# A hand-written order for the first stretch of a mixer kernel: loads, layer norms and the first projection on three engines

## The chip, the cores and the metric

The kernel runs on one core of one Trainium2 chip. The metric is the device time of one launch in microseconds (us), the median of several runs; smaller is better.

## The reference, cut to what matters

One layer: a token mixer (HGRN2 and GLA scans over 512 latent and 256 context tokens of width 1024), then a PEER expert layer. The change touches only the way to the first scan:

```python
m_l = jax.nn.silu(c) @ w_ada[i] + b_ada[i]
m_c = jax.nn.silu(c_ctx) @ w_ada[i] + b_ada[i]
...
u_l = modulate(x, sh1_l, sc1_l) @ w_in[i]     # modulate: layer_norm(x) * (1 + scale) + shift
u_c = modulate(xc, sh1_c, sc1_c) @ w_in[i]
```

The latent tokens x and the context tokens xc are normalized, scaled and shifted by the modulation columns, and projected by w_in.

## The kernel before, in words

`Net.mixer` opens with a stretch that ends when the first head unit's projections are begun; the body (project, scan) follows. Six token blocks of 128 rows (4 of x, numbers 2 to 5, and 2 of ctx, numbers 0 and 1) go through `first_norm`: a load into one of 4 buffers `xin` (L280), statistics on VectorE (L119, L125), the inverse deviation `rsa` by two ScalarE activations (L127, L128), the normalization on VectorE (L283), 8 TensorE transposes into two PSUM tiles `pT` (L288), two ScalarE copies to `xt` (L289). `mods_first` computes the modulation columns `m1` in 4 groups of 256 columns of shift and scale: 4 weight loads of 512 KB per group (`wada1`, 8 buffers, L173), 8 matmuls into `pmr` (L178), a VectorE copy `mrow` (L180), 4 tiny matmuls `pm` (L183), the sum with the bias column `b1` (L185). The bias is a load of 8 KB (L167), to whose scale half VectorE adds 1 (L168). `modulate_first` makes the input's high and low halves `hTh` (ScalarE, L296) and `hTl` (VectorE, L298, L299) for two of 8 slices k per group, latent and context apart. `w_slab` splits a weight slab `wraw` in the same way into `wh` (ScalarE, L308) and `wl` (VectorE, L309). `begin` multiplies, for each k, the latent tokens (2 matmuls of 512 columns into `pr`, 12 of 256 into `pt`) and the context tokens (5 of 256) with the first token slabs; after it the Z transposes (L364) and the first slab projection `pc` run. `scan_consts` makes masks and lower bounds for the scans.

Order: all engines work off their own queue in order. In this stretch of the kernel before, a list scheduler chose the order on each engine from the dependences. Loads are issued by SP, all on one queue, and each load waits for a semaphore of one of 8 lanes: it is issued only when the load eight before it has landed.

Of the kernel before, what the change touches and what calls it, by code (L numbers as in the profile page):

```python
# [21 lines left out]
TC = 256  # L22
# [9 lines left out]
class Net:  # L32
    def __init__(self, tc, a):
        self.tc, self.nc, self.a = tc, tc.nc, a

# [17 lines left out]
    def scan_consts(self, c, tmp):  # L53
        nc, a = self.nc, self.a

        si = tmp.tile([128, 64], I32, name="si")
# [19 lines left out]

        z = c.tile([128, 2, 4], F32, name="lbz")
        nc.sync.dma_start(z, a["hg_lb"])
# [17 lines left out]

        self.w2 = c.tile([64, 2, 256], F32, name="w2")
        nc.vector.memset(self.w2, 0.0)
        for i in (0, 32):
            nc.sync.dma_start(self.w2[i:i + 16, 0, :], a["w_gk2"][0])  # L100
            nc.sync.dma_start(self.w2[i + 16:i + 32, 1, :], a["w_gk2"][1])
        self.bgk = c.tile([128, 2, 2], F32, name="bgk")
        nc.sync.dma_start(self.bgk, a["b_gk"])
# [41 lines left out]
    def mods_first(self, pers, pool, ps):  # L145

        nc, a = self.nc, self.a
        t1 = pool.tile([128, 8, 2], F32, name="cct1")  # L150
        t2 = pool.tile([128, 8, 2], F32, name="cct2")
        sil = pool.tile([128, 8, 32], F32, name="sil")
        sc = sil[:, :, 0:2]
        nc.vector.memset(sil, 0.0)
        self.log_sigmoid(sc, self.cc, t1, t2)
        nc.scalar.activation(sc, sc, AF.Exp)
        nc.vector.tensor_tensor(sc, sc, self.cc, op=OP.mult)

        si = pool.tile([128, 2], I32, name="seli")
        nc.gpsimd.iota(si, pattern=[[-1, 2]], base=0, channel_multiplier=1)  # L160
        nc.vector.tensor_scalar(si, si, 31, None, op0=OP.bitwise_and)
        sel = pool.tile([128, 2], F32, name="sel")
        nc.vector.tensor_copy(sel, si)
        nc.vector.tensor_scalar(sel, sel, 0.0, None, op0=OP.is_equal)
        self.m1 = pers.tile([128, 16, 2], F32, name="m1")
        bias = pool.tile([128, 4, 2, 2], F32, name="b1")
        nc.sync.dma_start(bias, a["b1col"])  # L167
        nc.vector.tensor_scalar(bias[:, :, 1], bias[:, :, 1], 1.0, None, op0=OP.add)  # L168
        for g in range(4):
            yield  # L170
            ws = [pool.tile([128, 2, 512], F32, name="wada1", bufs=8) for _ in range(4)]
            for i, w in enumerate(ws):
                nc.sync.dma_start(w, a["w_ada1"][g][:, i * 2:i * 2 + 2])  # L173
            yield
            p = ps.tile([128, 512], F32, name="pmr", bufs=1)
            for k in range(8):
                j = k % 4 * 32
                nc.tensor.matmul(p[j:j + 32, :], sil[:, k, :], ws[k // 2][:, k % 2, :], start=k < 4, stop=k > 3)  # L178
            mrow = pool.tile([128, 512], F32, name="mrow", bufs=2)
            nc.vector.tensor_copy(mrow, p)  # L180
            pm = ps.tile([128, 4, 2], F32, name="pm", bufs=1)
            for m in range(4):
                nc.tensor.matmul(pm[:, m, :], mrow[:, m * 128:(m + 1) * 128], sel, start=m == 0, stop=m == 3)  # L183
            for i in range(2):
                nc.vector.tensor_tensor(self.m1[:, 8 * i + 2 * g:8 * i + 2 * g + 2], pm[:, 2 * i:2 * i + 2],  # L185
                                        bias[:, g, i, :, None].to_broadcast([128, 2, 2]), op=OP.add)

# [88 lines left out]
    def first_norm(self, pool, ps, xt, b):  # L276
# [6 lines left out]
        nc.vector.tensor_scalar(x, x, mu, rs, op0=OP.subtract, op1=OP.mult)  # L283
        for g in range(2):
# [6 lines left out]
    def modulate_first(self, pool, xt, ks, *parts):  # L291
        nc = self.nc
        for k in ks:
            for i, j, s in parts:
                sc, sh = self.m1[:, 8 + k, s:s + 1], self.m1[:, k, s:s + 1]
                nc.scalar.activation(self.hTh[:, k, i:j], xt[:, k, i:j], AF.Identity, bias=sh, scale=sc)  # L296
                h = pool.tile([128, T], F32, name="hT", bufs=3)[:, :j - i]
                nc.vector.tensor_scalar(h, xt[:, k, i:j], sc, sh, op0=OP.mult, op1=OP.add)  # L298
                nc.vector.tensor_tensor(self.hTl[:, k, i:j], h, self.hTh[:, k, i:j], op=OP.subtract)  # L299


    def w_slab(self, src):
        shape = [128] + list(src.shape[1:])
        raw = self.wp.tile(shape, F32, name="wraw", bufs=2)
        self.nc.sync.dma_start(raw, src)
# [4 lines left out]
        return hi, lo  # L310

    def token_slabs(self, u):
        return [self.w_slab(self.a["w_tf"][u, :, i * 4:(i + 1) * 4, :]) for i in range(2)]
# [280 lines left out]
    def begin(self, u, ps, slabs, wr):  # L594
# [7 lines left out]
        for k in range(8):  # L602
            wh, wl = (t[:, k % 4, :] for t in slabs[k // 4])
            ctx = lambda: self.mm3(both[:, 0, :], wh[:, 0:128], wl[:, 0:128], self.hTh[:, k, 0:TC], self.hTl[:, k, 0:TC],
                                   k == 0, k == 7)
            if k < 7:
                ctx()
            for p, sl in ((pc, slice(0, TC)), (pl, slice(TC, TA))):
                for i, h in enumerate((self.hTh, self.hTl)):
                    nc.tensor.matmul(p, wr[:, k, :], h[:, k, sl], start=p is pl and k + i == 0,  # L610
                                     stop=p is pl and k + i == 8)
            if k == 7:
                ctx()
# [4 lines left out]
            if k % 2:  # L618
                yield
# [149 lines left out]
    def mixer(self, es):  # L769
# [13 lines left out]
        with tc.tile_pool(name="first", bufs=1) as fp, tc.tile_pool(name="fps", bufs=2, space=PSUM) as fps:  # L783
# [6 lines left out]
            mods = self.mods_first(self.c, fp, fps)  # L790
            norm = [self.first_norm(fp, fps, xt, b) for b in (2, 3, 4, 5, 0, 1)]
            step = lambda *gens: [next(g, None) for g in gens]
            lat, ctx = (TC, TA, 0), (0, TC, 1)
            step(*norm[:4], mods, mods)
            self.scan_consts(self.mp, fp)
            step(norm[0], norm[1], norm[4], norm[5])
            raw = fp.tile([128, 8, 32], F32, name="wr")
            nc.sync.dma_start(raw, self.a["w_r"])
            slabs = self.token_slabs(seq[0])
            wr = fp.tile([128, 8, 64], F32R, name="wrs")  # L800
            nc.scalar.activation(wr[:, :, 0:32], raw, AF.Copy)
            nc.vector.tensor_tensor(wr[:, :, 32:64], raw, wr[:, :, 0:32], op=OP.subtract)
            self.ahead = {}
            begin = self.begin(seq[0], fps, slabs, wr)
            step(norm[2], norm[3], mods, mods)
            self.modulate_first(fp, xt, range(0, 2), lat)
            step(norm[4], norm[5])
            self.modulate_first(fp, xt, range(0, 2), ctx)
            for g in (1, 2, 3):
                step(mods, begin, mods)  # L810
                self.modulate_first(fp, xt, range(2 * g, 2 * g + 2), lat, ctx)
            step(begin, begin)
# [5 lines left out]
        LEAD = 1.145  # L818
        while proj:
            if pp < ps + LEAD:  # L820
                pp = advance(proj, pp)
            elif m2 and pm < ps:
                m2 = m2 if next(m2, None) else None
# [557 lines left out]
```

## Time and profile before

| what | value |
|---|---|
| median of 3 runs (lowest, highest) | 1765.1 us (1762.88, 1768.2) |
| the profiled execution's own time | 1758.76 us |
| its span, first to last instruction | 1756.6 us |
| mean granted TensorE clock, share of full | 0.987 |
| TensorE matmul busy in the span | 97% |
| VectorE, ScalarE busy in the span | 82%, 47% |

The timelines below give for each instruction (or merged run of equal ones) its start from the span's beginning, its duration, engine, line, operation, output and inputs; in square brackets stands the engine's idle time before it and what ended it. Matmuls are pipelined: the next one starts before the shown end of the last, so the distance of two starts is the price of one.

### The profile page before, as it was taken

The numbers are of one execution on the slowest core, as the hardware profiler recorded it, in microseconds if no ns is written. First come the engines' busy times: TensorE is split into PE (matmuls) and PEld (weight loads), VectorE is DVE, ScalarE is ACT, GpSimd is POOL, SyncE is SP. The second block draws the span as 40 slices with busy tenths as digits, with TensorE's granted clock in tenths as the row PEclk, the third lists the DMA queues.
The fourth block names the chain that finished last, engine by engine and source line by source line (L and its number), as shares of the span: only waits on it lengthen the run. The fifth ranks groups of instructions, "written<-read, shape, count | busy, mean of one in ns | idle before, by whom it ended". The sixth has DMA issues, their size and how long they took to land. (4 is left out here: it accounts for less than half of the span.)

```text
span 1756.6 us, 28197 instructions
## 1 busy us (share of the span) xinstructions
PE 1699.8 (97%) x10501; PEld 1486.9 (85%) x10501; DVE 1447.2 (82%) x2917; ACT 833.2 (47%) x1417; POOL 406.7 (23%) x286
## 2 busy tenths in 40 slices
PE   6999999989999999999999999999999999999997
PEld 3888877877778999999998999999999998888886
DVE  6688988877779999999996878777777786776768
ACT  4677677655133355676674333333333333333332
POOL 0000000000023102238422544443444342111000
PEclk8999999999989999999999999999999999999999
DMA  8444435242322257989999999989999989999862
GB/s 321 122 127 162 139 96 182 95 179 101 108 73 85 73 152 290 332 298 322 332 333 355 368 341 351 323 304 334 325 309 338 321 299 309 351 332 305 270 217 96
DMA packets 174811, 428.99 MB, mean 244 GB/s; under 512 B 14993, under 2 KB 78801, under 8 KB 170578
## 3 DMA queue, kind: packets, MB, share of 16 engines
q1 hardware_dynamic: 137234, 290.87, 48.5%
q0 software_dynamic: 36864, 134.23, 21.8%
q8 instruction: 82, 1.34, 0.3%
q10 hardware_dynamic: 576, 2.10, 0.3%
q14 instruction: 55, 0.45, 0.1%
HBM read 378.38 MB, written 48.76 MB: 243 GB/s over the span
## 5 line engine op out<-in xcount | busy, mean ns | idle before, releaser
L139 PE MATMUL pH<-hh,uh 128*128 128x384 f32 x1024 | 350.3, 342 | 1.1 <-ACT gels L1111 1.1
L141 PE MATMUL pH<-hh,ul 128*128 128x384 f32 x1024 | 347.7, 340 | 1.5 <-DVE ul L1098 1.5
L140 PE MATMUL pH<-hl,uh 128*128 128x384 f32 x1024 | 347.0, 339 | 0.0
L139 PE MATMUL y<-vh,ah 128*128 128x512 f32 x768 | 302.8, 395 | 2.9 <-ACT ah L1137 2.9
L140 PE MATMUL y<-vl,ah 128*128 128x512 f32 x768 | 301.5, 393 | 0.1
L141 PE MATMUL y<-vh,al 128*128 128x512 f32 x768 | 301.5, 394 | 0.0
L1098 DVE TENSOR_TENSOR vl<-vr,vh 128x1024 fp32r<-128x1024 f32 x128 | 156.7, 1224 | 151.7 <-ACT vh L1096 150.7
L1167 POOL DMA_INDIRECT erow<-in_u_dram,ix x128 | 187.8, 1467 | 370.4 <-DVE scr L1176 219.1
L1167 POOL DMA_INDIRECT erow<-in_v_dram,ix x128 | 185.4, 1448 | 327.3 <-DVE yg L1184 179.8
L1096 ACT ACTIVATE vh<-vr 128x1024 fp32r<-128x1024 f32 x128 | 135.1, 1057 | 195.2 <-issue 125.9
L1137 ACT ACTIVATE ah<-gel 128x384 fp32r<-128x384 f32 x128 | 66.8, 524 | 276.6 <-DVE gel L1134 273.6
L139 PEld LDWEIGHTS pH<-hh,uh 128*128 128x128 f32 x1024 | 192.4, 188 | 3.8 <-ACT gels L1111 1.4
L140 PEld LDWEIGHTS pH<-hl,uh 128*128 128x128 f32 x1024 | 192.8, 188 | 2.7
L141 PEld LDWEIGHTS pH<-hh,ul 128*128 128x128 f32 x1024 | 192.4, 188 | 2.6 <-DVE ul L1098 2.4
L1096 ACT ACTIVATE uh<-ur 128x1024 fp32r<-128x1024 f32 x128 | 135.0, 1056 | 121.2 <-PE pH L140 75.3
L141 PEld LDWEIGHTS y<-vh,al 128*128 128x128 f32 x768 | 144.9, 189 | 33.6
L139 PEld LDWEIGHTS y<-vh,ah 128*128 128x128 f32 x768 | 144.7, 188 | 33.0 <-ACT ah L1137 3.4
L140 PEld LDWEIGHTS y<-vl,ah 128*128 128x128 f32 x768 | 144.9, 189 | 30.6 <-DVE vl L1098 0.5
L1098 DVE TENSOR_TENSOR ul<-ur,uh 128x1024 fp32r<-128x1024 f32 x128 | 155.6, 1216 | 16.0 <-PE pH L141 13.9
L1184 DVE SCALAR_TENSOR_TENSOR yg<-erow,act,yg 128x1024 f32<-128x1024 f32 x127 | 162.2, 1277 | 0.1
L1176 DVE SCALAR_TENSOR_TENSOR scr<-erow,h 128x1024 bf16<-128x1024 f32 x128 | 155.8, 1218 | 0.0
L139 PE MATMUL pc<-hTh,wh 128*128 128x512 f32 (+1 forms) x304 | 109.5, 360 | 0.9 <-ACT V L407 0.7
(367 smaller groups left out, 3047.0 us busy)
## 6 DMA issues: line engine op xcount, KB each, us to landing
ur<-in_uT_dram SPq DMA_DIRECT2D x128, 512.0 KB
vr<-in_v_dram SPq DMA_DIRECT2D x128, 512.0 KB
Gd<-stage SPq DMA_DIRECT2D x24, 1024.0 KB
Gn<-Gd SPq DMA_DIRECT2D x16, 1536.0 KB
wraw<-in_w_cf_dram SPq DMA_DIRECT2D x24, 512.0 KB
wada<-in_w_ada_dram SPq DMA_DIRECT2D x48, 256.0 KB
Hd<-gels SPq DMA_DIRECT2D x56, 192.0 KB
gel<-Hd SPq DMA_DIRECT2D x56, 192.0 KB
```

The lines of the kernel that those rows point to most:

```text
L139: mm(out, lh, rh, start=start, stop=False)
L140: mm(out, lh, rl, start=False, stop=False)
L141: mm(out, ll, rh, start=False, stop=stop)
L1096: nc.scalar.activation(hi, raw, AF.Copy)
L1098: sub = eng.tensor_tensor(lo, raw, hi, op=OP.subtract)
L1137: nc.scalar.activation(ah, g, AF.Copy)
L1167: nc.gpsimd.indirect_dma_start(out=e, out_offset=None, in_=a[src], in_offset=bass.IndirectOffsetOnAxis(ap=self.ix[:, j:j + 1], axis=0))
L1176: nc.vector.scalar_tensor_tensor(scr, e, 1.0, h2, op0=OP.mult, op1=OP.mult, accum_out=dots[:, j:j + 1])
L1184: nc.vector.scalar_tensor_tensor(y, e, act[:, j:j + 1], y, op0=OP.mult, op1=OP.add)
```

## The change

TensorE, VectorE and ScalarE follow the program's own order in the stretch (`manual_schedule`), and the program is rewritten step by step. Loads: the raw vector `wr` and the two first token slabs are issued straight behind the four x blocks, and the bias and the modulation weights behind them; the second ctx block and parts of `scan_consts` move among the weights. `begin` hands out two functions, `latent(k)` and `context(k)`, which the program calls as the columns become ready. Both slabs are split before the first modulation group is copied. The masks and bounds of `scan_consts` come after the modulation of latent slices 2 and 3. `modulate_first` makes all high halves and products first and the low halves after them. The first 8 body steps are held behind the last of these instructions and loads. The rest of the kernel is the same.

```diff
@@ mods_first
-        for g in range(4):
-            yield
+        def load(g):
             ws = [pool.tile([128, 2, 512], F32, name="wada1", bufs=8) for _ in range(4)]
...
+        loaded = [load(0)]
+        yield
+        loaded.append(load(1))
+        yield
+        for g in range(4):
+            ws = loaded[g]
...
@@ modulate_first
-                nc.vector.tensor_tensor(self.hTl[:, k, i:j], h, self.hTh[:, k, i:j], op=OP.subtract)
+                todo.append((self.hTl[:, k, i:j], h, self.hTh[:, k, i:j]))
+        for out, h, high in todo:
+            lo = nc.vector.tensor_tensor(out, h, high, op=OP.subtract)
@@ mixer
-            step(*norm[:4], mods, mods)
-            self.scan_consts(self.mp, fp)
...
+            with tc.manual_schedule(engines={*engines}):
+                step(*(norm[b] for b in (2, 3, 4, 5)))
+                raw = fp.tile([128, 8, 32], F32, name="wr")
+                nc.sync.dma_start(raw, self.a["w_r"])
+                raws = self.token_raws(seq[0])
+                mods = self.mods_first(self.c, fp, fps)
+                consts = self.scan_consts(self.mp, fp)
+                wr = fp.tile([128, 8, 64], F32R, name="wrs")
+                step(mods, norm[2], norm[2], norm[3], norm[3], consts)
+                step(norm[4], norm[0], norm[1], mods)
...
+                step(norm[4], norm[5])
+                slabs = [self.split(raws[0])]
+                step(mods, norm[5])
...
+                slabs.append(self.split(raws[1]))
+                begin = self.begin(seq[0], fps, slabs, wr)
+                latent, context = next(begin)
+                step(mods, mods)
+                mod((0, 1), lat)
+                step(norm[0], norm[1])
+                latent(0)
+                latent(1)
+                step(norm[0], norm[1])
+                mod((0, 1), ctx)
+                step(mods, mods)
+                context(0)
+                context(1)
+                step(mods)
+                mod((2, 3), lat)
+                step(consts)
+                mod((2, 3), ctx)
+                latent(2)
+                step(mods)
+                latent(3)
...
+                for k in (6, 7):
+                    latent(k)
+                    context(k)
```

Three places of the built program, first the queue of loads on SP, from its start. Before:

```order
L785 DMA cc<-in_ccol_dram 128x16
L280 DMA xin<-in_x_dram 128x1024 x4
L167 DMA b_130<-in_b1col_dram 128x16
L173 DMA wada_133<-in_w_ada_dram 128x1024
L173 DMA wada_134<-in_w_ada_dram 128x1024
```

Now:

```order
L822 DMA cc<-in_ccol_dram 128x16
L294 DMA xin<-in_x_dram 128x1024 x4
L835 DMA wr<-in_w_r_dram 128x256
L329 DMA wraw<-in_w_tf_dram 128x1024 x2
L169 DMA b_139<-in_b1col_dram 128x16
L174 DMA wada_142<-in_w_ada_dram 128x1024
```

The bias `b` stood right behind the x blocks and now stands behind `wr` (128 KB) and two slabs of 512 KB.

VectorE up to the second normalization (`sel` is a small constant, `sta` and `mva` the statistics). Before, the bias (L168) stood behind the second normalization:

```order
L119 BN_STATS sta<-xin 128x6
L64 CAST xf<-xo 128x64
L283 TENSOR_SCALAR xin<-xin,mva,rsa 128x1024
L168 TENSOR_SCALAR b_130<-b_130 128x4x2
L69 TENSOR_SCALAR mlo<-xf 128x64
```

Now:

```order
L166 TENSOR_SCALAR sel<-sel 128x2
L170 TENSOR_SCALAR b_139<-b_139 128x4x2
L121 BN_STATS sta<-xin 128x6 x2
L127 BN_AGGR mva<-sta 128x2
L297 TENSOR_SCALAR xin<-xin,mva,rsa 128x1024
L121 BN_STATS sta<-xin 128x6 x2
L127 BN_AGGR mva<-sta 128x2
L297 TENSOR_SCALAR xin<-xin,mva,rsa 128x1024
```

The instruction on the bias now heads the statistics of all blocks.

ScalarE over the x blocks. Before, the deviation of the second block (L127, L128) stood ahead of the first block's copies (L289):

```order
L127 ACTIVATE rsa<-mva,eps 128x1
L128 ACTIVATE rsa<-rsa 128x1
L127 ACTIVATE rsa<-mva,eps 128x1
L128 ACTIVATE rsa<-rsa 128x1
L289 ACTIVATE xt<-pT 128x4x128 x2
```

Now:

```order
L129 ACTIVATE rsa<-mva,eps 128x1
L130 ACTIVATE rsa<-rsa 128x1
L304 ACTIVATE xt<-pT 128x4x128 x2
L129 ACTIVATE rsa<-mva,eps 128x1
L130 ACTIVATE rsa<-rsa 128x1
L304 ACTIVATE xt<-pT 128x4x128 x2
```

Each block's deviation now stands behind the copies of the block before it.

## Rows read from the trace of the kernel before

**Rows 1.** Windows: start:end, length, busy (count) of PE, PEld, DVE, ACT, POOL; PEclk, DMA.

```profile
26.50:31.40 4.90, 4.90 (x20) 2.64 (x20) 3.50 (x6) 2.83 (x6) 0.00 (x0) 0.50 1.02 400
...
64.70:90.10 25.40, 25.40 (x146) 22.38 (x146) 19.32 (x37) 20.36 (x31) 0.00 (x0) 1.00 0.63 185
90.10:93.00 2.90, 0.47 (x3) 0.19 (x2) 2.90 (x7) 2.90 (x7) 0.00 (x0) 0.98 0.18 30
93.00:96.40 3.40, 3.40 (x17) 3.40 (x18) 3.40 (x6) 1.14 (x4) 0.00 (x0) 0.52 0.74 232
```

**Rows 2.** Timeline of TensorE in the stretch and at its end.

```profile
8.68 4.02 PE L288 MATMUL pT<-ident,xin 128*128 128x128 f32 x16 [8.68 <-DVE ident L47]
...
14.46 1.09 PE L288 MATMUL pT<-ident,xin 128*128 128x128 f32 x8
...
26.49 1.97 PE L288 MATMUL pT<-ident,xin 128*128 128x128 f32 x8 [6.06 <-DVE xin L283]
...
40.77 1.06 PE L178 MATMUL pmr<-wada,sil 128*32 128x512 f32 x8
...
46.30 0.95 PE L183 MATMUL pm<-sel,mrow 128*128 128x2 f32 x8
...
48.14 0.39 PE L610 MATMUL pr<-hTh,wrs 128*64 128x512 f32 x1
...
48.60 0.28 PE L139 MATMUL pt<-wh,hTh 128*128 128x256 f32 x1
48.72 0.29 PE L140 MATMUL pt<-wl,hTh 128*128 128x256 f32 x1
...
64.68 0.50 PE L139 MATMUL pc<-hTh,wh 128*128 128x512 f32 x1 [0.25 <-ACT G L376]
```

**Rows 3.** Timeline of SP: the issues of the 13th, 15th and 16th load.

```profile
8.83 0.32 SPq L101 DMA_DIRECT2D w<-in_w_gk_dram  x1
...
10.75 0.31 SPq L101 DMA_DIRECT2D w<-in_w_gk_dram  x1
12.04 0.35 SPq L103 DMA_DIRECT2D bgk<-in_b_gk_dram  x1
```

**Rows 4.** DMA packets of two stretches: first 3.1 to 7.8 us, then 7.8 to 9.2.

```profile
DMA packets 512, 1.90 MB, mean 404 GB/s; under 512 B 48, under 2 KB 48, under 8 KB 512
...
DMA packets 271, 0.46 MB, mean 331 GB/s; under 512 B 160, under 2 KB 160, under 8 KB 271
```

**Rows 5.** Timeline of VectorE in the stretch.

```profile
4.87 1.29 DVE L119 BATCH_NORM_STATS2 sta<-xin 128x6 f32<-128x512 f32 x2 [0.97 <-DMA xin<-in_x_dram]
...
7.04 0.80 DVE L283 TENSOR_SCALAR xin<-xin,mva,rsa 128x1024 f32<-128x1024 f32 x1
...
11.31 0.20 DVE L70 SCALAR_TENSOR_TENSOR mask<-xf,mlo 128x64 uint8<-128x64 f32 x1
...
14.82 0.81 DVE L283 TENSOR_SCALAR xin<-xin,mva,rsa 128x1024 f32<-128x1024 f32 x1
...
18.63 0.69 DVE L180 COPY mrow<-pmr 128x512 f32<-128x512 f32 x1 [2.38 <-PE pmr L178]
...
20.65 0.11 DVE L185 TENSOR_TENSOR m<-pm,b 128x4 f32<-128x4 f32 x1
...
21.92 0.68 DVE L299 TENSOR_TENSOR hTl<-hT,hTh 128x512 fp32r<-128x512 f32 x1
...
30.07 1.23 DVE L309 TENSOR_TENSOR wl<-wraw,wh 128x1024 fp32r<-128x1024 f32 x1 [1.36 <-ACT wh L308]
...
34.38 0.91 DVE L299 TENSOR_TENSOR hTl<-hT,hTh 128x256 fp32r<-128x256 f32 x2 [0.24 <-ACT hTh L296]
```

**Rows 6.** Timeline of ScalarE in the stretch.

```profile
6.43 0.29 ACT L127 ACTIVATE rsa<-mva,eps 128x1 f32<-128x1 f32 x1 [2.74 <-DVE mva L125]
...
10.69 0.60 ACT L289 ACTIVATE xt<-pT 128x512 f32<-128x512 f32 x1 [0.25 <-PE pT L288]
...
28.99 1.05 ACT L308 ACTIVATE wh<-wraw 128x1024 fp32r<-128x1024 f32 x1
```

More of the change, by code (lines that the diff above doesn't have):

```diff
@@ L310, in w_slab, with token_raws @@
         return hi, lo
+    def token_raws(self, u):
+        return [self.raw_slab(self.a["w_tf"][u, :, i * 4:(i + 1) * 4, :]) for i in range(2)]
     def token_slabs(self, u):
-        return [self.w_slab(self.a["w_tf"][u, :, i * 4:(i + 1) * 4, :]) for i in range(2)]
+        return [self.split(raw) for raw in self.token_raws(u)]
     def proj_c(self, slab, out_l, out_c, colmajor=False, scale=1.0):
@@ L601, in begin, with latent @@
         self.ahead[u] = [both[:, 0, :], *vg]
-        for k in range(8):
+        def latent(k):
             wh, wl = (t[:, k % 4, :] for t in slabs[k // 4])
[L604 to L613, printed above, removed]
+            for i, h in enumerate((self.hTh, self.hTl)):
+                nc.tensor.matmul(pl, wr[:, k, :], h[:, k, TC:], start=k + i == 0, stop=k + i == 8)
             for b in range(2, 6):
@@ L617, in begin, with context, value @@
                          k == 0 and b % 2 == 0, k == 7 and b % 2 == 1)
-            if k % 2:
-                yield
+        def context(k):
+            wh, wl = (t[:, k % 4, 0:128] for t in slabs[k // 4])
+            def value():
+                self.mm3(both[:, 0, :], wh, wl, self.hTh[:, k, 0:TC], self.hTl[:, k, 0:TC], k == 0, k == 7)
+            if k < 7:
+                value()
+            for h in (self.hTh, self.hTl):
+                nc.tensor.matmul(pc, wr[:, k, :], h[:, k, 0:TC], start=False, stop=False)
+            if k == 7:
+                value()
+        yield latent, context
         nc.scalar.activation(self.rT[:, TC:].rearrange("p (c r) -> p c r", r=8),
@@ L789, in mixer @@
             seq = (0, 1, 4, 2, 5, 3)
-            mods = self.mods_first(self.c, fp, fps)
-            norm = [self.first_norm(fp, fps, xt, b) for b in (2, 3, 4, 5, 0, 1)]
+            lat, ctx = (TC, TA, 0), (0, TC, 1)
+            mod = lambda ks, part: self.modulate_first(fp, xt, ks, part)
             step = lambda *gens: [next(g, None) for g in gens]
-            lat, ctx = (TC, TA, 0), (0, TC, 1)
-            step(*norm[:4], mods, mods)
-            self.scan_consts(self.mp, fp)
-            step(norm[0], norm[1], norm[4], norm[5])
@@ L797, in mixer @@
[L797 to L812, printed above, removed]
+            norm = {b: self.first_norm(fp, fps, xt, b) for b in range(6)}
+            engines = (mybir.EngineType.PE, mybir.EngineType.DVE, mybir.EngineType.Activation)
@@ new lines, in mixer @@
+            with tc.manual_schedule(engines={*engines}):
[8 more added lines that the diff above has]
+                step(norm[4], norm[0], norm[1], mods)
+                nc.scalar.activation(wr[:, :, 0:32], raw, AF.Copy)
+                step(norm[4], norm[5])
+                slabs = [self.split(raws[0])]
+                step(mods, norm[5])
+                nc.vector.tensor_tensor(wr[:, :, 32:64], raw, wr[:, :, 0:32], op=OP.subtract)
+                slabs.append(self.split(raws[1]))
+                self.ahead = {}
+                begin = self.begin(seq[0], fps, slabs, wr)
[17 more added lines that the diff above has]
+                latent(3)
+                step(mods)
+                context(2)
+                context(3)
+                step(mods)
+                mod((4, 5), lat)
+                mod((4, 5), ctx)
+                step(mods)
+                latent(4)
+                step(mods)
+                latent(5)
+                step(mods)
+                context(4)
+                context(5)
+                mod((6, 7), lat)
+                mod((6, 7), ctx)
+                for k in (6, 7):
+                    latent(k)
+                    context(k)
@@ L813, in mixer @@
+            step(begin)
         self.up = pool(el, "unit")
@@ L818, in mixer @@
         LEAD = 1.145
+        behind = 8
         while proj:
-            if pp < ps + LEAD:
+            if behind:
+                behind -= 1
+                with self.behind():
+                    pp = advance(proj, pp)
+            elif pp < ps + LEAD:
                 pp = advance(proj, pp)
             elif m2 and pm < ps:
-                m2 = m2 if next(m2, None) else None
+                with self.behind():
+                    m2 = m2 if next(m2, None) else None
                 pm += 0.165
```

51 lines of the change are left out of this document (36 added, 15 removed).

## The prediction

> **What bounds the kernel now.** I read the busy times by stretch first: from 64.7 to 90.1 us, the start of the body, TensorE is busy 25.40 of 25.40 us at full clock [rows 1]. So whatever moves the first slab projection `pc`, which starts at 64.68 [rows 2], moves the body behind it, and the question is when `pc` starts after the change. Then I read the timelines of the four queues ahead of it. TensorE: 16 transposes as soon as the first blocks are normalized (8.68), an idle gap of 6.06 us before the ctx transposes at 26.49, and after that hardly a gap up to 64.68 [rows 2]. That gap is what an order by hand could win, with the half clock behind it: from 26.5 to 31.4 the granted clock was 0.50 (1.2 GHz) [rows 1]; 8 transposes took 1.97 us there and 1.09 at 2.4 GHz [rows 2]. VectorE: statistics of the first block at 4.87, as soon as it has landed, normalizations at 7.04 and, the fourth, 14.82; first modulation columns done at 20.76 (20.65 + 0.11) [rows 5]. SP: a load is issued when the load eight before it has landed, so these issues date landings: the 13th at 8.83 is the landing of the fourth x block, the 15th and 16th at 10.75 and 12.04 are landings of two weight loads of 512 KB, 1.29 us apart [rows 3].
>
> **The change, step by step.** I follow the chain of what waits for what on the new order, with durations from rows.
>
> *1. The bias load.* It now stands behind `wr` and two slabs, and the VectorE instruction that adds 1 to it heads the statistics of every block. One queue serves its loads in order: before, the bias was issued at 3.08 behind the x blocks. In 3.1 to 7.8 us only 48 packets under 512 B moved, in the much shorter 7.8 to 9.2 us 160 [rows 4]. The bias is 128 small packets, so they moved with the end of the last x block. Now it lands at 8.83 plus a quarter of 1.3 for `wr`, two times 1.3 for the slabs and 0.2 for itself: 12.0. VectorE, which took its first statistics at 4.87, starts them at 12.0. All x blocks have been there since 8.83.
>
> By the Trainium skill's page "DMA: Bandwidth & Descriptors", section "Queues, rings and completion order", completion is not first-in first-out per issuing engine, so a small load could finish ahead of large ones; rows 4 speak against it here. By that rule step 1 would cost nothing (the first rival).
>
> *2. Four normalizations in series.* The first follows the statistics as before: 12.0 + (7.04 - 4.87) = 14.2 [rows 5]. For the others ScalarE's order decides: the deviation of a block now stands behind the copies of the block before it, and those wait for the transposes, which wait for the normalization. A period is: normalization 0.80 [rows 5], 8 transposes, second copy 0.60, two activations 0.29 + 0.20 [rows 6], four handovers of about 0.1. With transposes at half clock (4.02 / 2 = 2.0 [rows 2]) that is 4.2 to 4.3 us, at full clock (1.09) 3.3. I take 4.2, because TensorE comes from idle and has 2 us of work in each period; 3.3 is kept as the low end. The fourth normalization starts at 14.2 + 3 x 4.2 = 26.8 and ends at 27.6, where it started at 14.82 before.
>
> *3. To the first modulation columns.* Now both slabs are split ahead of `mrow`. Behind the fourth normalization: 8 transposes and second copy 1.9 (29.5; at half clock 0.9 more), `wh` of the second slab on ScalarE 1.05 [rows 6], `wl` 1.23, `mrow` 0.69 [rows 5], `pm` 0.95 [rows 2], sums 0.2 and handovers: columns at 33.8, 13.0 us later than the 20.76 of before. The weights land by about 17.2 (12.0 + 4 x 1.3), so they no longer set anything.
>
> *4. From the columns to* `pc`. Prices: latent(k) two starts of 0.23 (48.14 to 48.60) and 12 of 0.12 = 1.9; context(k) 5 x 0.12 = 0.6; four `pmr` matmuls 1.06 [rows 2]; columns to first low half 1.8 (20.76 to 22.60) [rows 5].
> - low half of slice 0 at 35.5. latent(0), latent(1): 3.8, plus 1.5 for a part at half clock, since TensorE was idle from about 29.7 (between 0 and the 2.4 that 4.9 us at half clock cost from 26.5 [rows 1]): 40.8.
> - The ctx norms start when VectorE is through the low halves (36.1) and take 3.0 each in series: 42.0. Second ctx transposes to 43.1, eight `pmr` to 45.2, context(0), (1) to 46.4, `pm` behind `mrow` to 47.4, columns 47.7, low half 49.4: TensorE is idle for 2.
> - latent(2), four `pmr`, latent(3), four `pmr`: 5.9, to 55.3. context(2) waits: VectorE does the scan constants from 50.0, 26 small instructions of 0.2 [rows 5] and three trips to ScalarE, 6.0 in all, then product and low halves of ctx (0.73 + 0.91 [rows 5]): end of context(3) at 58.2, `pm` 59.2, columns 59.5, low half 61.2.
> - latent(4), four `pmr`, latent(5) 4.9: 66.1. `pm` 67.0, contexts 68.2, low half 69.0; the last two slices 5.0: 74.0. Then copies of the results, transposes and the first `pc`, 1.0, since context(7) now ends last: 75.0.
>
> Three times the first matmul of a latent part needs only the high half, which is there earlier: 0.2 each, and `pc` comes at 74.4 where it came at 64.68. What the change wins lies in here: 41 us from the columns to `pc` instead of 44, no `pmr` cut into pieces by other work, loads that no longer wait for late buffers. It does not pay for the 13.0 of steps 1 to 3.
>
> *Edits at nothing.* The moved small loads (bounds, gates) and the later ctx and weight loads: the first ctx load waits for the first block's transposes (17.0) and lands some 4 later; at 1.3 per load the weights of the second group are in by about 29, and TensorE asks for them at 43. Holding the first 8 body steps back: they stand there anyway. Apart from a few neighbours swapped, the body's order is the same, so the shift is carried to the end.
>
> **The sum.** 74.4 - 64.68 = 9.7 us. Against the profiled execution's 1758.76 that is 1768.5. The runs' median is 1765.1, so I forecast 1774.8 us, 0.55% slower. 0.3% (5.3 us) is about what a measurement of this kernel can tell from no change.
>
> **Rivals.**
> - *The bias overtakes the slabs* and is there with the first x block. VectorE then starts at 4.87; the fourth normalization ends at 7.04 + 12.6 + 0.8 = 20.4, 7.2 earlier, and the sum falls to 2.5: 1767.6, no change that can be told. It decides if the bias lands before the first block. For it: 8 KB is little. Against: rows 4. 6%.
> - *Full clock.* If TensorE gets 2.4 GHz between the bursts, each of three periods costs 0.9 less and the 1.5 at latent(0) goes: 9.7 - 4.2 = 5.5, 1770.6, just over the bound. For it: after two bursts without a pause and some `pmr`, transposes took 1.09 from 14.46 [rows 2]. Against: the first ones after idling were slow both times (8.68, 26.49). 14%.
> - *The body takes it back.* TensorE is idle for all but 0.47 us from 90.1 to 93.0 and then has 3.4 us at a clock of 0.52 [rows 1], 2.4 + 1.7 = 4.1 lost to a wait for ScalarE, where a slab's `wh` of 1.05 stood in the way. If that closes, 5.6 is left: 1770.7. 6%.
> - *Everything for the change*: the bias early, full clock, and the gap at 90 closed: 2.5 - 4.2 - 2.4 = -4.1, 1761.0, faster, but by less than can be told. 2%.
>
> On the other side, each of TensorE's new idle places (47.4 to 49.4, 59.2 to 61.2) may halve the clock again, at 1.7 each as from 93.0 to 96.4, and the transposes of step 3 may run at half clock, 0.9: 9.7 + 4.3 = 14.0.
>
> **How the numbers follow.** The forecast keeps 70%, and 2% are left for what I have not seen, counted as faster. All the bounds together give 2.5 to 14.0 us, which is 1767.6 to 1779.1; with the spread of the runs shown (some 2.5 us either way) the range 1767.5 to 1780 leaves out about 2 in 10. Slower by over 0.3% (over 1770.4): the forecast's 70% and half of the two cases that end at 1770.6 and 1770.7, 10%, less 1% for its own low tail: 79%. Within 0.3%: the other half, the overtaking bias (6%), the last rival (2%) and that tail, 19%. Faster: 2%.
>
> **What would show it.** Right: VectorE's statistics of the first block start at about 12, with the wait put down to the load of `b`; the four x normalizations start some 4.2 us apart (3.3 would show the full clock); the first `mrow` stands behind the second `wl` at about 32; TensorE begins latent(0) at about 35; `pc` starts at 73 to 76; what follows up to the end has the time it had before. Wrong: statistics at 5 (step 1 falls), normalizations less than 3 us apart (step 2), or `pc` after 74 and an end that is not later (the body took it back).

## The result and the profile after the change

The change takes 1774.68 us (median of 20 runs, 1766.07 to 1784.72), the kernel before 1765.39 (20 runs on the same chip, 1759.60 to 1773.25). The ratio is 1.0057, 95% interval [1.0043, 1.0072]: slower by 0.57%, where 0.55% was forecast. The profiled execution of the change took 1781.17 us (span 1779.2) and lies 6.5 above its median; that of the kernel before lay 6.6 below its own. So 22.4 us lie between the two profiled executions and 9.3 between the medians, and I read the two traces by stretches, not by their ends.

The busy times hardly differ (the page of the change; TensorE had 1699.8 before):

```profile
PE 1710.8 (96%) x10501; PEld 1495.2 (84%) x10501; DVE 1449.9 (81%) x2917; ACT 833.5 (47%) x1417; POOL 410.8 (23%) x286
```

VectorE of the change, the rows that answer to [rows 5] (start us, us, engine, line, operation, and in brackets the idle time ahead with what ended it):

```profile
13.21 0.17 DVE L170 TENSOR_SCALAR b<-b 128x8 f32<-128x8 f32 x1 [8.70 <-DMA b<-in_b1col_dram]
13.29 1.28 DVE L121 BATCH_NORM_STATS2 sta<-xin 128x6 f32<-128x512 f32 x2
15.41 0.81 DVE L297 TENSOR_SCALAR xin<-xin,mva,rsa 128x1024 f32<-128x1024 f32 x1 [0.60 <-ACT rsa L130]
19.34 0.81 DVE L297 TENSOR_SCALAR xin<-xin,mva,rsa 128x1024 f32<-128x1024 f32 x1 [1.67 <-ACT rsa L130]
...
27.18 0.81 DVE L297 TENSOR_SCALAR xin<-xin,mva,rsa 128x1024 f32<-128x1024 f32 x1 [1.67 <-ACT rsa L130]
...
32.77 0.68 DVE L192 COPY mrow<-pmr 128x512 f32<-128x512 f32 x1
35.32 0.23 DVE L198 TENSOR_TENSOR m<-pm,b 128x4 f32<-128x4 f32 x2 [1.87 <-PE pm L196]
```

VectorE stands still for 8.70 us until the bias is there, and starts the statistics at 13.29 where it started at 4.87. The normalizations are 3.92 apart, each behind a wait for ScalarE's `rsa`; the fourth starts at 27.18 (14.82 before), and the first columns are done at 35.55 (20.76).

TensorE of the change, answering to [rows 2]:

```profile
16.28 1.97 PE L303 MATMUL pT<-ident,xin 128*128 128x128 f32 x8 [16.28 <-DVE xin L297]
20.20 1.97 PE L303 MATMUL pT<-ident,xin 128*128 128x128 f32 x8 [1.95 <-DVE xin L297]
...
28.05 1.97 PE L303 MATMUL pT<-ident,xin 128*128 128x128 f32 x8
...
33.51 1.77 PE L196 MATMUL pm<-sel,mrow 128*128 128x2 f32 x8 [2.39 <-DVE mrow L192]
36.51 0.69 PE L639 MATMUL pr<-hTh,wrs 128*64 128x512 f32 x1 [1.23 <-ACT hTh L312]
...
77.08 0.50 PE L141 MATMUL pc<-hTh,wh 128*128 128x512 f32 x1
...
103.32 0.33 PE L515 MATMUL pkt<-ident,K 128*128 128x128 f32 x1 [0.51 <-ACT K L502]
104.41 0.44 PE L398 MATMUL pt<-ident,Z 128*128 128x128 f32 x2 [0.77 <-ACT Z L395]
...
116.20 0.83 PE L521 MATMUL pkv<-V,KT 128*128 128x128 f32 x6
...
188.84 0.49 PE L521 MATMUL pkv<-V,KT 128*128 128x128 f32 x2 [0.91 <-DVE S L532]
```

All four bursts of transposes take 1.97, what 8 transposes took at half clock [rows 2], with 1.95 of idling ahead of the second and 1.96 ahead of the third; `pm` takes 1.77 for 0.95. `pc` starts at 77.08, 12.40 later than before. The two short waits at 103 and 104 are the place where the kernel before idled from 90.1 to 93.0 [rows 1].

In the body, ScalarE makes the scan's keys `K`, TensorE transposes them (`pkt`), and `pkv`, their product with the values, is the scan's first product; VectorE sums the `pkv` into the state `S`. In the kernel before, TensorE has these rows there:

```profile
91.86 0.33 PE L481 MATMUL pkt<-ident,K 128*128 128x128 f32 x1 [1.67 <-ACT K L468]
...
106.42 0.83 PE L487 MATMUL pkv<-V,KT 128*128 128x128 f32 x6
```

Windows of the change (start:end, length, busy of PE, PEld, DVE, ACT, POOL; clock; DMA), the first from `pc` to the first `pkv`, the second further on:

```profile
77.10:116.20 39.10, 37.82 (x247) 34.52 (x248) 33.80 (x63) 31.08 (x52) 0.00 (x0) 1.00 0.51 161
190.00:204.00 14.00, 14.00 (x51) 9.64 (x52) 9.71 (x25) 8.88 (x16) 0.00 (x0) 0.52 0.56 179
```

From `pc` to the first `pkv` the kernel before took 41.7 us (64.68 to 106.4), with the clock at 0.52 for part of it [rows 1]; the change takes 39.1 at full clock. So 2.6 of the 12.4 come back, and `pkv` is 9.8 later, close to the 9.3 between the medians. Most of the rest of the 22.4 comes behind it: TensorE works from 190 to 204 at a clock of 0.52, which the kernel before does not do in that place, and the first `pq`, the queries of the expert layer, starts 19.3 later (518.0 for 498.7). What that stretch is, the last part tells.

### The profile page after: what moved, and what is told of

Read it like the earlier page. It is cut to its first block, busy times and chain, and to the rows that moved or that the text cites. A ratio compares the mean times of both kernels' runs of the same rounds, so it can differ in the third digit from the quotient of the medians.

```text
span 1779.2 us, 28200 instructions
## 1 busy us (share of the span) xinstructions
PE 1710.8 (96%) x10501; PEld 1495.2 (84%) x10501; DVE 1449.9 (81%) x2917; ACT 833.5 (47%) x1417; POOL 410.8 (23%) x286
## 5 line engine op out<-in xcount | busy, mean ns | idle before, releaser
L1248 POOL DMA_INDIRECT erow<-in_v_dram,ix x128 | 189.3, 1479 | 322.0 <-DVE yg L1265 179.3
```

What stands on the lines that cost most here:

```text
L1248: nc.gpsimd.indirect_dma_start(out=e, out_offset=None, in_=a[src], in_offset=bass.IndirectOffsetOnAxis(ap=self.ix[:, j:j + 1], axis=0))
```

## The experiments

Every kernel ran in 6 to 12 timed runs beside 23 to 35 of the kernel before on the same chip (one chip for e1 to e4, a second for e5 to e8, a third for e9 and e10). The table has, from one profiled execution of each, the start of the fourth x normalization, the end of the first columns, the time from there to the first `pc`, from `pc` to the first `pkv`, the start of that `pkv` (all us), and the ratio to the kernel before with its 95% interval. The plain ratio of the medians differs from that ratio by up to 0.0023 (e1: 1.0035), so the last column does not tell kernels apart that lie 0.002 from each other.

| kernel | 4th norm. | columns | to pc | to pkv | pkv at | ratio |
|---|---|---|---|---|---|---|
| before | 14.82 | 20.76 | 43.9 | 41.7 | 106.4 | 1 |
| the change | 27.18 | 35.55 | 41.5 | 39.1 | 116.2 | 1.0057 [1.0043, 1.0072] |
| e1 bias behind x | 23.02 | 30.30 | 41.5 | 38.9 | 110.7 | 1.0012 [0.9988, 1.0036] |
| e2 the 1 later | 18.97 | 25.80 | 41.5 | 39.4 | 106.8 | 1.0018 [0.9995, 1.0042] |
| e3 statistics ahead | 21.66 | 31.16 | 41.5 | 41.5 | 114.1 | 1.0023 [0.9997, 1.0049] |
| e4 both | 13.85 | 22.90 | 41.5 | 39.4 | 103.7 | 0.9975 [0.9955, 0.9996] |
| e5 warm | 31.03 | 43.22 | 41.5 | 41.0 | 125.7 | 1.0098 [1.0068, 1.0128] |
| e6 scheduler | 16.55 | 21.67 | 39.4 | 39.2 | 100.3 | 0.9986 [0.9960, 1.0011] |
| e7 not held | 26.35 | 34.75 | 43.9 | 42.3 | 121.0 | 1.0060 [1.0038, 1.0082] |
| e8 reordered | 13.84 | 20.72 | 39.8 | 41.5 | 102.0 | 0.9958 [0.9941, 0.9976] |
| e9 warm, less | 24.31 | 31.70 | 41.5 | 38.8 | 112.0 | 1.0024 [0.9997, 1.0051] |
| e10 reordered, warm | 13.69 | 20.51 | 37.4 | 38.9 | 96.8 | 0.9956 [0.9929, 0.9983] |

**e1: the bias back behind x.**

```diff
                 step(*(norm[b] for b in (2, 3, 4, 5)))
+                self.b1 = fp.tile([128, 4, 2, 2], F32, name="b1")
+                nc.sync.dma_start(self.b1, self.a["b1col"])
                 raw = fp.tile([128, 8, 32], F32, name="wr")
...
-        bias = pool.tile([128, 4, 2, 2], F32, name="b1")
-        nc.sync.dma_start(bias, a["b1col"])
+        bias = self.b1
```

> The bias is issued right behind the four x loads again, as before the change; nothing else is moved. Theory (the late bias holds the statistics, and what it costs there is carried to the end): it lands with the end of the fourth x block, at about 9.2 us where it landed at 13.19, so the statistics, the four normalizations and all behind them come 4.0 us earlier: fourth normalization at 23.2 instead of 27.18, first pc at 73 instead of 77.08, and the time about 4 us (0.23%) below that of the change: ratio to the kernel before 1.003. Rival A (something later sets pc, such as the weights or the ctx blocks, and eats the 4 us): normalizations 4 earlier, pc still at 76 to 77, ratio 1.005 to 1.006. Rival B (the load is not the cause): statistics still start at 13.

The statistics start at 9.14, the fourth normalization 4.2 earlier than in the change, `pc` at 71.82, 5.3 earlier (4.0 expected; the transposes behind the fourth block ran partly at full clock). So both rivals fall at `pc`. The ratio's interval, [0.9988, 1.0036], holds the 1.003 of the theory and not the 1.005 of rival A.

**e2: the 1 added behind the first** `mrow`.

```diff
-        nc.vector.tensor_scalar(bias[:, :, 1], bias[:, :, 1], 1.0, None, op0=OP.add)
...
             nc.vector.tensor_copy(mrow, p)
+            if g == 0:
+                nc.vector.tensor_scalar(bias[:, :, 1], bias[:, :, 1], 1.0, None, op0=OP.add)
             yield
```

> The bias is loaded as late as in the change, but the VectorE instruction that adds 1 to it stands behind the first mrow copy instead of ahead of the statistics. Theory: the statistics start with the first x block, at 4.9 to 5.6 (the sigmoid's instructions may stand in the way), 7.6 to 8.3 us earlier than in the change; the normalizations stay 3.9 apart, so the fourth comes at about 19.5 and pc at 69 to 70; time 7 to 8 us below the change, ratio to the kernel before 1.000 to 1.002. Rival A (the first weights, landing at 17 to 18, or the ctx loads take the place of the bias): fourth normalization at 19.5, but pc not before 73, ratio 1.003 or more. Rival B (what the change lost lies in the body, not ahead of pc): pc at 70 and the ratio still at 1.005.

VectorE of this kernel:

```profile
5.08 1.29 DVE L121 BATCH_NORM_STATS2 sta<-xin 128x6 f32<-128x512 f32 x2 [0.42 <-DMA xin<-in_x_dram]
...
11.13 0.81 DVE L298 TENSOR_SCALAR xin<-xin,mva,rsa 128x1024 f32<-128x1024 f32 x1 [1.67 <-ACT rsa L130]
15.05 0.81 DVE L298 TENSOR_SCALAR xin<-xin,mva,rsa 128x1024 f32<-128x1024 f32 x1 [1.20 <-ACT rsa L130]
```

One instruction of 0.17 us moved, the load left where it was: the statistics start 8.2 earlier, and `pc` at 67.31, 9.8 earlier than in the change. The normalizations keep their 3.92, so the series does not hang on the bias. The ratio is 1.0018; 1.0057 is outside its interval.

**e3: the statistics ahead.** `first_norm` gets a yield between statistics and normalization (two buffers for `sta`, `mva`, `rsa`), and the steps are called so that a block's statistics stand ahead of the transposes of the block before:

```diff
-                step(mods, norm[2], norm[2], norm[3], norm[3], consts)
-                step(norm[4], norm[0], norm[1], mods)
+                step(mods, norm[2], norm[3], norm[2], norm[2], norm[4], norm[3], norm[3], consts)
+                step(norm[5], norm[4], norm[0], norm[1], mods)
```

> The series is broken and the bias left late: the statistics of a block, and ScalarE's two activations on its deviation, stand ahead of the transposes and copies of the block before it. Theory: statistics still start at 13.2; VectorE then needs 1.3 + 0.1 of statistics and 0.8 of normalization per block, so the x normalizations come 2 to 2.6 us apart instead of 3.92, the fourth at about 22 instead of 27.18, and pc at about 72; ratio to the kernel before 1.003. Rival A (TensorE's half clock on the transposes sets the pace, 1.97 for each block): they come about 3.5 apart and the gain is 1 us. Rival B (later waits absorb it): normalizations at 22, pc at 76 or 77, ratio as for the change, 1.0057.

The normalizations start at 15.62, 17.73, 20.32 and 21.66, 2.0 apart on the mean though the first three bursts of transposes still took 1.94 to 1.97: the series was the order of VectorE and ScalarE, as step 2 said, and rival A falls. `pc` came at 72.62, 4.5 earlier, of which 0.5 is the bias's earlier landing here. `pkv` gained only 2.1, because this execution idled 1.58 + 0.76 us in the body and lost the clock there, as the kernel before does. The ratio's interval, [0.9997, 1.0049], has the theory's 1.003 inside and the change's 1.0057 outside.

**e4: both edits.**

> The two before together: the 1 is added behind the first mrow copy, and statistics stand ahead of the transposes of the block before. Theory: statistics from about 5, four normalizations done by about 15 to 16 as in the kernel before (15.6), and all of the 12.4 us that pc lost comes back: pc at 65 to 66. The first pkv stood 9.8 us later in the change with pc 12.4 later, so the body wins 2.6: pkv at 104 to 105 where the kernel before has it at 106.4, and a time 1 to 3 us below the kernel before, ratio 0.998 to 1.000. Rival A (with the blocks early, the first weights and the split of the second slab, 1.05 + 1.23 us, set the first modulation columns at 24 or later): pc at 68 to 69, ratio 1.001. Rival B (the order behind the columns is what costs): pc at 70 or later.

```profile
4.96 1.29 DVE L121 BATCH_NORM_STATS2 sta<-xin 128x6 f32<-128x512 f32 x2 [0.37 <-DMA xin<-in_x_dram]
...
13.85 0.81 DVE L299 TENSOR_SCALAR xin<-xin,mva,rsa 128x1024 f32<-128x1024 f32 x1 [0.58 <-ACT rsa L130]
...
19.70 1.23 DVE L342 TENSOR_TENSOR wl<-wraw,wh 128x1024 fp32r<-128x1024 f32 x1 [1.18 <-ACT wh L341]
20.84 0.68 DVE L191 COPY mrow<-pmr 128x512 f32<-128x512 f32 x1
```

With the start of the kernel before restored (fourth normalization 13.85 for 14.82), `pc` is at 64.35, `pkv` at 103.7, and the kernel is 0.25% faster than the kernel before, [0.9955, 0.9996]. So the change's loss is those two places, and without them the rest of the change wins. Here `wl` of the second slab holds `mrow`, and the columns come at 22.90 (20.76 before).

**e5: TensorE kept at work.** Matmuls of the identity with itself, without use:

```diff
+                def spin(n):
+                    p = fps.tile([64, T], F32, name="pr", bufs=1)
+                    for _ in range(n):
+                        nc.tensor.matmul(p[:, 0:128], self.ident[:, 0:64], self.ident, start=True, stop=True)
```

> TensorE gets work without use in its idle places: matmuls of the identity with itself, 128 columns each, into a bank that latent(0) clears later: 70 ahead of the first transposes, 12 behind each of the first three blocks' transposes, 24 behind the last and the first pmr. Nothing else is moved; VectorE still starts at about 13. Theory of the clock (the half clock on the transposes, on pm and on latent(0) is a price of TensorE's idling): the granted clock is 2.4 GHz at the transposes, 1.09 for 8 instead of 1.97, the normalizations come 3.0 to 3.1 apart instead of 3.92, the fourth at 24.6 instead of 27.18, pm takes 0.95 instead of 1.77 and latent(0) keeps full clock: pc at 72 to 73 instead of 77.08, ratio to the kernel before 1.002 to 1.003. Rival A: the clock does not follow such work, or falls again in the waits left: period 3.9, pc at 77, ratio 1.0057. Rival B: the clock is full but the added work gets in the way: pc at 75, ratio 1.0045.

```profile
4.42 16.88 PE L841 MATMUL pr<-ident 128*64 128x128 f32 x140 [4.42 <-DVE ident L48]
21.23 1.09 PE L303 MATMUL pT<-ident,xin 128*128 128x128 f32 x8
22.25 2.83 PE L841 MATMUL pr<-ident 128*64 128x128 f32 x24
25.02 1.09 PE L303 MATMUL pT<-ident,xin 128*128 128x128 f32 x8
```

The clock followed (1.09), but each of my matmuls is two records and 0.24 us, twice what I had counted: the first 70 held the first transposes from 15 to 21.23, the 12 took 2.83 of each period. `pc` came at 84.73 and the ratio is 1.0098: rival B, worse than its 1.0045. My sizes were wrong, so e9 does it again.

**e9: the same with 32, 6 and 8.**

> The change with TensorE kept at work again, in amounts that fit the waits: one such matmul took 0.24 us in the run before (140 passes in 16.88 us for 70), so now 32 ahead of the first transposes (7.7 us from 4.4 on), 6 behind each of the first three blocks (1.4 of the 1.95 us of idling) and 8 behind the last pmr. Theory of the clock: transposes 1.09 instead of 1.97, normalizations 3.0 to 3.1 apart, the fourth 2.6 us earlier relative to the first than in the change, last transposes and pm 0.9 and 0.8 shorter, latent(0) at full clock or close to it: pc at 71.5 to 73 instead of 77.08, ratio to the kernel before 1.002 to 1.003. Rival A (VectorE and ScalarE set the pace at full clock as well): normalizations 3.5 or more apart, pc at 75. Rival B (the clock falls in the waits left, 0.5 us in each period): transposes at 1.97 again, pc at 77.

```profile
15.60 1.09 PE L303 MATMUL pT<-ident,xin 128*128 128x128 f32 x8 [1.85 <-DVE xin L297]
16.63 1.52 PE L841 MATMUL pr<-ident 128*64 128x128 f32 x12
18.70 1.09 PE L303 MATMUL pT<-ident,xin 128*128 128x128 f32 x8 [0.55 <-DVE xin L297]
...
22.08 1.09 PE L303 MATMUL pT<-ident,xin 128*128 128x128 f32 x8 [0.84 <-DVE xin L297]
```

Normalizations 3.09 to 3.39 apart, the fourth 9.57 behind the first (11.77 in the change), `pc` at 73.22 and a ratio of 1.0024, about as the theory has it. Of the 3.9 us at `pc` 0.7 is VectorE's earlier start in this execution (12.62 for 13.29); 3.2 is what the half clock had cost, and it came from TensorE's idling: nothing else was moved. By the Trainium skill's page "TensorE: Matmul & The Clock Gate", section "What's actually happening", a block sets the array's clock by how busy TensorE has been recently; 1.09 here for 1.97 in the change agrees.

**e6: the scheduler's order.** The change with `ExitStack()` in place of the order by hand:

```diff
-            with tc.manual_schedule(engines={*engines}):
+            with ExitStack():
```

> The change without its order by hand: loads, parts and everything else as in the change, but TensorE, VectorE and ScalarE are ordered by the scheduler, which puts the 1 on the bias behind the fourth statistics, the deviations ahead of the copies, and splits the first slab early. Theory (the order by hand lost the time; the order of loads did not): bias still lands at 12.3 to 13.2, statistics from 4.9, fourth normalization by about 15, first modulation columns at 21 to 22, pc at 61 to 64, ratio to the kernel before 0.996 to 0.999. Rival A (slabs and bias ahead of the first weights cost by themselves): columns at 25 or later, pc at 68 or later, ratio 1.002 or more.

```profile
4.90 1.29 DVE L121 BATCH_NORM_STATS2 sta<-xin 128x6 f32<-128x512 f32 x2 [0.91 <-DMA xin<-in_x_dram]
...
14.64 0.17 DVE L170 TENSOR_SCALAR b<-b 128x8 f32<-128x8 f32 x1
...
16.55 0.81 DVE L297 TENSOR_SCALAR xin<-xin,mva,rsa 128x1024 f32<-128x1024 f32 x1
...
21.44 0.23 DVE L198 TENSOR_TENSOR m<-pm,b 128x4 f32<-128x4 f32 x2 [1.07 <-PE pm L196]
```

The first 14 loads are the same in the same order; of those behind them the second ctx block, issued at 22.54 in the change, comes ahead of the weights. `pc` is at 61.09, 16 us ahead of the change and 3.6 ahead of the kernel before. The ratio, 0.9986 [0.9960, 1.0011], excludes the change's 1.0057. The order by hand lost the time; slabs and bias ahead of the first weights cost nothing that shows (rival A falls).

**e7: the first 8 body steps not held back** (`behind = 0`).

> The change with none of the first 8 body steps held behind the hand-ordered stretch (8 set to 0); the stretch itself is as in the change. Theory, as the prediction has it: holding them costs and wins nothing, pc at 77 (76 to 78), the first pkv 39 behind it, ratio to the kernel before 1.0057 (1.004 to 1.007). Rival: the holding is what closed the body's gap of the kernel before (pkv 41.7 behind pc there, 39.1 in the change): pkv 41 to 42 behind pc, ratio 1.007 or more.

Here the theory was wrong. VectorE and TensorE of this kernel:

```profile
61.64 1.22 DVE L340 TENSOR_TENSOR wl<-wraw,wh 128x1024 fp32r<-128x1024 f32 x1
62.78 1.28 DVE L317 TENSOR_TENSOR hTl<-hT,hTh 128x512 fp32r<-128x512 f32 x2
```

```profile
63.52 0.69 PE L639 MATMUL pr<-hTl,wrs 128*64 128x512 f32 x1 [1.49 <-DVE hTl L317]
```

Not held, the body's first `wl` slips in front of the low halves of slices 4 and 5; TensorE waits 1.49 and has a clock of 0.50 from 63.5 to 66.7. From the columns to `pc` it took 43.9, as in the kernel before, not 41.5; and `pkv` came 42.3 behind `pc`, about the 41 to 42 of the rival. In the time itself, 1.0060 [1.0038, 1.0082], it does not show against the 1.0057 of the change.

**e8: reordered.** What e1 to e4 showed, put into an order (to e4's edits; the scan constants in three pieces in VectorE's waits, and the statistics of both ctx blocks ahead of their normalizations):

```diff
-                slabs.append(self.split(raws[1]))
...
                 mod((2, 3), lat)
...
                 mod((2, 3), ctx)
...
+                slabs.append(self.split(raws[1]))
+                for k, ks in ((2, (4, 5)), (4, (6, 7))):
+                    latent(k)
+                    step(mods, mods)
+                    latent(k + 1)
+                    step(mods)
+                    mod(ks, lat)
+                    context(k)
+                    context(k + 1)
+                    mod(ks, ctx)
```

> A stretch ordered by hand by what the runs have shown: as the kernel with both edits (statistics ahead, 1 added behind mrow), and: the second slab is split behind the modulation of slices 2 and 3, not ahead of mrow (2.3 us of VectorE and ScalarE, of which 1.6 lay on the way to mrow); statistics of both ctx blocks ahead of their normalizations; both halves of pmr ahead of the second latent part of a pair and pm right behind it, so that the context parts cover the way from pm to the next high half (waits of TensorE there: 1.23, 1.17, 0.9 and 0.5, with 1 to 2 us of half clock behind them); scan constants in VectorE's waits. Theory: pc at 59 to 60, 4.5 to 5.5 ahead of the 64.35 of the kernel with both edits, and the time as much below it: ratio to the kernel before 0.994 to 0.996. Rival A (the second group of weights, landed at 27 to 28.6, sets the second columns): only the 1.6 ahead of mrow is won, pc at 62.5, ratio 0.997. Rival B (the body's loads are late when pc comes earlier): pc at 60, but pkv more than 41 behind it, ratio 0.997.

TensorE in windows of this kernel:

```profile
22.00:26.00 4.00, 3.88 (x16) 3.22 (x16) 3.93 (x9) 0.91 (x4) 0.00 (x0) 0.50 0.89 303
...
34.00:38.00 4.00, 4.00 (x21) 3.67 (x21) 3.96 (x12) 3.21 (x5) 0.00 (x0) 0.59 0.87 311
```

Columns at 20.72 and `pc` at 60.50, 3.9 ahead of e4 where 4.5 to 5.5 was expected: behind the two waits left around `pm` the clock was 0.50 and 0.59. The ratio is 0.9958 [0.9941, 0.9976], inside the forecast.

**e10: e8 with TensorE kept at work in those waits** (3 such matmuls ahead of the first `pm`, 5 behind it, 3 ahead of the second; half of the second `pmr` ahead of the ctx transposes).

> The reordered stretch with matmuls without use in its two waits: 3 ahead of the first pm, 5 behind it, 3 ahead of the second pm; and the first half of the second pmr ahead of the ctx transposes, not behind the first of them. There the granted clock was 0.50 from 22 to 26 us and 0.59 from 34 to 38 in the reordered kernel. Theory of the clock: full clock from 16 us on; latent(0) and latent(1) take 4.0 instead of 6.8 us, of which VectorE's ctx normalizations (done at 26.6 and 27.3) give back about 1; second pm at 31 instead of 33.36, latent(2) at 33.3 instead of 36.22, 1.6 more behind it: pc at 56 to 57 instead of 60.50, and ratio to the kernel before 0.993 to 0.994 where the reordered kernel had 0.9958. Rival A (the clock falls all the same): pc at 60, ratio 0.996. Rival B (pc earlier, but the body waits for ScalarE and loads): pc at 57, pkv more than 42 behind it, ratio 0.996.

```profile
15.00:26.00 11.00, 10.64 (x79) 7.35 (x73) 9.95 (x28) 4.42 (x9) 0.00 (x0) 1.00 0.98 374
26.00:36.00 10.00, 9.00 (x68) 6.11 (x68) 8.77 (x29) 6.73 (x16) 0.00 (x0) 1.00 0.92 324
```

Full clock in both stretches, `pc` at 57.92 (expected 56 to 57), `pkv` at 96.8, 9.6 ahead of the kernel before. The ratio, 0.9956 [0.9929, 0.9983], holds the 0.993 to 0.994 expected and also e8's 0.9958: whether the last 5.2 us at `pkv` reach the end, these runs do not settle. In the profiled execution they do not: it is the slowest of the twelve (1772.39), has a stretch at half clock behind `pkv` as the change has, and starts `pq` at 495.4 where e8 does at 495.2. Both kernels are faster than the kernel before, and so than the change: their whole intervals lie below 1.

## Why the prediction was right

The forecast was +9.7 us at `pc`, carried to the end; measured are +12.4 at `pc`, +9.8 at `pkv`, +9.3 in the medians. The sign, the place and the mechanism up to `pc` stand: step 1 by e1 and e2, step 2 by e3 and e9, and together by e4. That the size fits so closely is luck: two errors cancel, 2.7 too little at `pc` (77.08, past the 73 to 76 named beforehand) and 2.6 that came back behind it.

- *Step 1*, the bias lands at 12.0 and VectorE starts then: 13.19. The first of its 16 parts was complete at 11.94; in this execution the last came 1.25 later. In e3, e5, e7 and e9, with the same loads up to the bias, VectorE got it at 12.39 to 12.75. The first rival (the bias overtakes) is out: in no run that issues it behind the slabs did it land ahead of them. The landings kept the order of the issues (slabs 11.65 and 13.02, bias 13.19, first weights 14.39). The rule of the Trainium skill's page "DMA: Bandwidth & Descriptors", section "Queues, rings and completion order", that completion is not first-in first-out per issuing engine, gave the rival less than the prediction took from it: the page draws it for a later load on one DMA engine against an earlier one on 16, and the bias's completion came in 16 parts, as those of the slabs did.
- *Step 2*, a period of 4.2: 3.92, so the fourth normalization at 27.18 for 26.8; the later start and the shorter period nearly cancel. The half clock taken for the series was right, and the second rival (full clock) failed on its condition, not on its price: e9 makes its condition true and gets 3.2 us of the 4.2.
- *Step 3*, columns at 33.8: 35.55. Behind the fourth normalization I had put 7.0 us, and it took 8.37, because the last transposes (1.97 for 1.09) and `pm` (1.77 for 0.95) ran slower too, 1.70 together; the other items took 0.3 less than I had put. The first I had named as a bound of 0.9, the second not.
- *Step 4*, 40.6 from columns to `pc`: 41.5, so 2.4 won against the 43.9 of before, not 3.3. Seven kernels with this order have 41.5 to within 0.1, late or early. An item that I costed at nothing carries this: e7 shows that without holding the body's steps back those 2.4 are gone; they do not stand there "anyway".
- *What follows up to the end has the time it had before*: wrong by 2.6 at `pkv`. The third rival, at 6% and with 4.1, is what happened in part: TensorE's wait for `K` went from 1.67 to 0.51, and the clock stayed at 1.00. But its cause is only in small part the one the rival named. In the kernel before, ScalarE splits a slab between two pieces of `K`; in the change `wh` comes later. ScalarE of the kernel before:

```profile
88.02 0.51 ACT L465 ACTIVATE K<-LF,cb 128x256 f32<-128x256 f32 x1 [0.60 <-DVE cb L455]
88.43 1.04 ACT L308 ACTIVATE wh<-wraw 128x1024 fp32r<-128x1024 f32 x1
...
91.42 0.39 ACT L468 ACTIVATE K<-LF,tb 128x128 f32<-128x128 f32 x1
```

and of the change:

```profile
99.84 0.51 ACT L499 ACTIVATE K<-LF,cb 128x256 f32<-128x256 f32 x1 [0.66 <-DVE cb L489]
100.25 0.68 ACT L502 ACTIVATE K<-LF,tb 128x128 f32<-128x128 f32 x2
...
102.87 0.39 ACT L502 ACTIVATE K<-LF,tb 128x128 f32<-128x128 f32 x1
```

These are a few of the rows that I had dismissed as "neighbours swapped". From the first piece to the one that TensorE waits for it is 3.40 before and 3.03 in the change, so the swap is worth some 0.4 of the 1.16 by which the wait shrank. Another 0.6 comes from ahead of `cb`: the first piece starts 23.34 behind `pc` before and 22.76 in the change. VectorE, which makes `cb`, waits for weights (`wada`) of the second modulation. VectorE of the kernel before, and of the change:

```profile
74.73 0.69 DVE L215 SCALAR_TENSOR_TENSOR wada<-wada,silrow 128x512 f32<-128x512 f32 x1 [2.32 <-DMA wada<-in_w_ada_dram]
82.01 0.69 DVE L215 SCALAR_TENSOR_TENSOR wada<-wada,silrow 128x512 f32<-128x512 f32 x1 [0.59 <-DMA wada<-in_w_ada_dram]
```

```profile
87.02 0.69 DVE L229 SCALAR_TENSOR_TENSOR wada<-wada,silrow 128x512 f32<-128x512 f32 x1 [1.61 <-DMA wada<-in_w_ada_dram]
93.15 0.69 DVE L229 SCALAR_TENSOR_TENSOR wada<-wada,silrow 128x512 f32<-128x512 f32 x1 [0.16 <-DMA wada<-in_w_ada_dram]
```

Nine kernels have the change's order on ScalarE in this place. Between `pc` and `K` they differ in how long VectorE waits for those loads, and TensorE's wait for `K` follows it one by one (us):

| | e10 | e9 | e1 | the change | e4 | e2 | e5 | e8 | e3 |
|---|---|---|---|---|---|---|---|---|---|
| VectorE waits for `wada` | 1.12 | 1.23 | 1.43 | 1.77 | 2.22 | 2.29 | 2.40 | 2.99 | 3.22 |
| TensorE waits for `K` | 0.19 | 0.20 | 0.31 | 0.51 | 0.77 | 0.80 | 0.86 | 1.39 | 1.58 |
| `pc` to `pkv` | 38.9 | 38.8 | 38.9 | 39.1 | 39.4 | 39.4 | 41.0 | 41.5 | 41.5 |

The three on the right have a clock of 0.96 in that stretch, the other six 1.00. In all nine SP issues these loads at the same times behind `pc`; the one that VectorE waits for longest is complete between 9.35 (e10) and 10.92 us (e3) behind `pc`. So the gain of 2.6 hangs in good part on a load's landing and is not firm. Why it lands sooner in one profile than in the next, by the kernel or by chance, was not tried.

The stage times carry the result of nearly every kernel: the shift of `pkv` against 106.4, over 1765 us, gives 1.0056 for the change, 0.9985 for e4, 1.0109 for e5, 0.9965 for e6 and 0.9946 for e10, each inside the measured interval; for e1, e2, e3, e8 and e9 it gives 1.0024, 1.0002, 1.0044, 0.9975 and 1.0032, likewise inside. Only e7's 1.0083 lies just above its interval.

## What to carry to other kernels

In an order written by hand, the small load is the dangerous one: look at what each engine's first instruction behind it waits for, and put the use of a late small operand right ahead of where its result is needed. Put the short instruction that releases the next round (here ScalarE's deviation) ahead of the long ones that finish this round, or rounds that could overlap run in series. And where the first bound is a stage's start, read the landmarks of stages (columns, `pc`, `pkv`) of the two traces rather than their ends: with 1765 us and a spread of 14 to 19 us from run to run, they show a shift of 2 us, and the end of one execution does not. They have a spread of their own, though: with the same loads ahead of it the bias landed between 12.2 and 13.2 us, so with one profile of each kernel a shift below 1 us counts only where its cause stands in the rows.

## What the runs showed of the hardware

- Work without use paid for itself here where TensorE would have idled between dependent steps: 11 small matmuls in e10 brought the clock from 0.50 and 0.59 to 1.00 in two stretches, and `pc`, together with one reordered half of `pmr`, forward by 2.6 us. Sized wrongly (e5) it costs more than it saves.
- The spread of the runs goes with the clock. In each kernel the longer runs tend to be those with the lower mean granted clock (0.981 to 0.989 over the 20 runs of the change); a line through all runs, with a level for each kernel, has about 1.5 us for each 0.001. One such stretch can be seen: at 70 to 90 us behind the first `pkv` three of the twelve profiles (the change, e6, e10) work some 14, 10 and 14 us at half clock, and the other nine do not. Ahead of it TensorE had waited for VectorE's `S` for 0.91, 0.67 and 1.11 us; in the other nine that wait was between nothing and 0.73. So the wait's length alone does not decide it (0.67 in e6 with the half clock, 0.69 in e7 and 0.73 in e5 without), and why the wait differs stays open.
- The clock's column does not show the half clock of the first transposes: e8 has 1.00 in the window from 8.6 to 17 us, where the first 8 transposes took 1.97, as at 0.50 in the kernel before [rows 1, 2]. There only the durations tell.
